# Two parts of the moving operand through one weight load: 512-column matmuls in the FFN and convolution projections

## The chip, the cores and the metric

The kernel runs on one core of a Trainium2 chip. The metric is the device time of one execution in microseconds (us). Before the change it is 1189.55 us, the median of 3 runs (1188.36 to 1194.43).

A core has five engines with a queue each. TensorE (PE) multiplies a stationary operand of 128x128 (the weights, loaded by a separate instruction, PEld) with a moving operand of up to 512 columns and writes into PSUM, a memory of 8 banks with 512 fp32 values in each of 128 partitions. VectorE (DVE), ScalarE (ACT) and GpSimd (POOL) do elementwise work. SyncE (SP) issues the transfers from HBM. An engine takes its instructions strictly in the order of its queue.

## The reference

Four residual layers over 256 positions of width 1024. Each layer is a token mixer (short convolution, recurrent block, latent attention, short convolution) and a SwiGLU FFN of width 2816:

```python
def short_conv_mixer(xn, w_in, w_conv, w_out):
    b_gate, c_gate, h = jnp.split(xn @ w_in, 3, axis=-1)
    y = b_gate * causal_depthwise_conv(c_gate * h, w_conv)
    return y @ w_out

def swiglu_ffn(xn, w_gu, w_down):
    gate, up = jnp.split(xn @ w_gu, 2, axis=-1)
    return (jax.nn.silu(gate) * up) @ w_down

h = x
for i in range(DEPTH):                       # DEPTH = 4
    xn = rms_norm(h, mix_norm[i])
    y = ...                                  # mixer i mod 3
    h = h + y
    h = h + swiglu_ffn(rms_norm(h, ffn_norm[i]), ffn_w_gu[i], ffn_w_down[i])
```

All of it is fp32.

## The kernel before

**Layout.** Activations stand transposed: features on the 128 partitions, the 256 positions (`S`) along the free dimension. The residual stream is `xt`, 8 tiles (`KD`) of 128x256. The FFN's hidden vector is 22 such tiles (`KF`).

**Precision.** An fp32 product is made of three matmuls of a shorter type (fp32r). Each operand is split into a high part (a copy in fp32r) and a low part (what the copy lost): `whi`, `wlo` for weights, `xh`, `xl` for the normalised stream, `yh`, `yl` for the convolution's result, `hh`, `hl` for the hidden vector. `mm3` (L166 to L168) adds high times high, high times low and low times high into the same PSUM columns; the low times low is left out. So each block of 128x128 weights takes three matmuls of 256 columns, each with its own weight load, two of them of the same `whi` block.

**Weights.** `load_w` fetches a tile of 128 x 1024 (four blocks deep, 256 output features wide) on SP's queue, ACT makes `whi` (L79), DVE makes `wlo` (L80). Up to 8 tiles are held ahead; there are 6 raw buffers, 8 of `whi` and 8 of `wlo`, so a new `whi` waits until TensorE has used the tile eight places earlier. Every weight is used once.

**FFN.** The loop over `jp` (11 steps per layer, 44 in all) makes 256 hidden features a step. A step takes four weight tiles: gate and up for the first four blocks of the stream, then gate and up for the last four. Two PSUM banks are in use: bank `j` holds the gate in columns 0 to 255 and the up branch in 256 to 511. Then, for each `j`, DVE multiplies the bank by the norm factor (L966, 512 columns), ACT applies SiLU (L968), POOL multiplies by the up branch (L969), and `split` makes `hh` on ACT (L179) and `hl` on DVE (L180). The down projection is `project_out` in layers 0 to 2 (four output pairs `mp`, each 22 blocks deep and one bank wide) and `project_last` in layer 3, which has the positions as rows. After each pair `mp` one DVE addition of 512 columns brings the bank into `xt` (L293), and `epilogue` makes the new `xh` (ACT, L182), `xl` (DVE, L183), the squares (ACT, L239) and their sum `acc` (POOL, L244) for the next norm.

**Convolution.** The in-projection makes three parts in 12 groups, POOL, ACT and DVE make `y`, and `project_out` multiplies by `w_out`.

**Order.** The framework's scheduler sets each engine's instruction order from the dependencies; the code's own order is a guide to it. The PSUM pool of the projections has six banks (`mm`), a second pool has two (`mi`). A tile taken from the pool gets the bank that was taken six tiles earlier and waits until that one has been read.

Of the kernel before, what the change touches and what calls it, by code (L numbers as in the profile page):

```python
# [16 lines left out]
P = 128  # L17
# [30 lines left out]
KC = 4  # L48
# [5 lines left out]
def tile_trunk(ctx: ExitStack, tc: tile.TileContext, ins: dict, out: bass.AP):  # L54
# [9 lines left out]
    def ps_tile():  # L64
        return psum.tile([P, 512], F32, name="mm")
# [96 lines left out]
    def mm3(ps, a, b, start, stop):  # L162
# [59 lines left out]


    xt = st.tile([P, KD, S], F32, name="xt")
    xh = st.tile([P, KD, S], F32R, name="xh")
    xl = st.tile([P, KD, S], F32R, name="xl")
    acc = st.tile([P, S], F32, name="acc")
    rstd = st.tile([P, S], F32, name="rstd")

# [51 lines left out]
    def project_out(ktiles, rhs, gain, order=None, pss=None):  # L281
# [3 lines left out]
        for mp, k0, k in order or out_order(ktiles):  # L285
# [68 lines left out]

    def short_conv(li, l):
        with tc.tile_pool(name=f"cv{li}", bufs=2) as pool:
            yh = pool.tile([P, KD, S], F32R, name="yh", bufs=1)
            yl = pool.tile([P, KD, S], F32R, name="yl", bufs=1)

            at, rb, pend, g = (0, 1) if li else (2, 3), None, [], {}  # L360

            def conv(jp, cg, hg, bg):
                ch = pool.tile([P, 2, S + CW - 1], F32, name="ch")
                nc.gpsimd.memset(ch[:, :, :CW - 1], 0.0)
                nc.gpsimd.tensor_tensor(ch[:, :, CW - 1:], cg, hg, op=ALU.mult)
                y = pool.tile([P, 2, S], F32, name="y")
                for j in range(2):
                    m = 2 * jp + j

                    def cw(i):  # L370
                        o = o_cw + (l * CW + i) * KD + m
                        return c1[:, o:o + 1]

                    nc.scalar.activation(y[:, j], ch[:, j, 0:S], AF.Copy, scale=cw(0))
                    for i in range(1, CW):
                        nc.vector.scalar_tensor_tensor(y[:, j], ch[:, j, i:i + S], cw(i), y[:, j],
                                                       op0=ALU.mult, op1=ALU.add)
                nc.gpsimd.tensor_tensor(y, y, bg, op=ALU.mult)
                split((yh[:, 2 * jp:2 * jp + 2, :], yl[:, 2 * jp:2 * jp + 2, :]), y)

            for n, (jp, part) in enumerate((jp, part) for jp in range(KD // 2) for part in (1, 2, 0)):
                ps = ps_tile().rearrange("p (a s) -> p a s", s=S)
# [8 lines left out]
                while rb is not None and pend:  # L391
# [2 lines left out]
                    nc.vector.tensor_tensor(g[part], ps, rb, op=ALU.mult)  # L394
                    if part == 0:
                        conv(jp, g[1], g[2], g[0])
            project_out(KD, lambda k: (yh[:, k, :], yl[:, k, :]),
                        o_ffn + li * KD)

    def late_params(late):  # L400
        c2, (o_lcw, o_lcb, o_gab, o_gxb, o_lam) = columns("c2", [
# [536 lines left out]

    def ffn(li):
        with tc.tile_pool(name=f"ff{li}", bufs=2) as pool:  # L940
            hh = pool.tile([P, KF, S], F32R, name="hh", bufs=1)
            hl = pool.tile([P, KF, S], F32R, name="hl", bufs=1)
            rb = None
            for jp in range(KF // 2):
                if li == DEPTH - 1 and jp == 0:
                    xr = pool.tile([P, 2, D], F32, name="xr", bufs=1)
                if li == DEPTH - 1 and 4 <= jp < 4 + KD // 2:
                    by_position(xr, jp - 4)
                if (li, jp) == (0, 2):
                    late.extend(late_params(pool))  # L950
                pss = [ps_tile().rearrange("p (a s) -> p a s", s=S) for _ in range(2)]
                for k0 in range(0, KD, KC):
                    w = next_ws(2)
                    if jp == 0 and k0:
                        dg = norm_sums()
                    for k in range(KC):
                        for i, (hi, lo) in enumerate(w):
                            for j, ps in enumerate(pss):
                                sl = slice(j * P, (j + 1) * P)
                                mm3(ps[:, i, :], (hi[:, k, sl], lo[:, k, sl]), xk(k0 + k),  # L960
                                    start=(k0 + k == 0 and i == 0), stop=(k0 + k == KD - 1))
                for j, ps in enumerate(pss):
                    f = 2 * jp + j
                    rb = rb or norm_bcast(dg)
                    gu = pool.tile([P, 2, S], F32, name="gu")
                    nc.vector.tensor_tensor(gu, ps, rb, op=ALU.mult)  # L966
                    s = pool.tile([P, S], F32, name="s")
                    nc.scalar.activation(s, gu[:, 0], AF.Silu)  # L968
                    nc.gpsimd.tensor_tensor(s, s, gu[:, 1], op=ALU.mult)  # L969
                    split((hh[:, f, :], hl[:, f, :]), s)  # L970
            hidden = lambda k: (hh[:, k, :], hl[:, k, :])
            if li == DEPTH - 1:
                project_last(KF, hidden, xr)
            else:
                project_out(KF, hidden, o_mix + (li + 1) * KD)

    late = []
    short_conv(0, 0)
# [36 lines left out]
```

## Time and profile before

| | |
|---|---|
| median of 3 runs | 1189.55 us |
| profiled execution, its time | 1188.12 us |
| profiled execution, its span | 1186.3 us |
| TensorE busy | 1156.7 us (98%), 9475 matmuls |
| VectorE busy | 805.6 us (68%) |
| ScalarE busy | 609.0 us (51%) |
| GpSimd busy | 259.8 us (22%) |
| HBM read | 202.04 MB, 171 GB/s over the span |
| mean granted clock of TensorE | 0.993 |

The span is the stretch between the first and the last instruction of the trace; 1.8 us lie around it. A matmul's recorded duration (280 to 290 ns for 256 columns) covers its passage through the pipeline, so matmuls overlap; what one costs is the distance between the starts of two that follow each other. In the FFN's steps a matmul starts every 120 ns for stretches of tens of microseconds.

### The profile page before, as it was taken

How to read it: one execution, taken by the hardware profiler on the slowest of the kernel's cores; microseconds unless marked ns; L12 is line 12 of the kernel's file. 1: busy time of each engine (PE TensorE's matmuls, PEld its weight loads, DVE VectorE, ACT ScalarE, POOL GpSimd, SP SyncE). 2: the span in 40 equal slices, each digit the busy share in tenths (PEclk: the TensorE clock that was granted, in tenths of full speed). 3: DMA queues.
4: the chain of work that ended last, by engine and by line, in shares of the span. 5: the costliest groups of instructions: out<-in, count | busy, mean ns of one | idle time of the engine just before them, and what ended most of it. 6: DMA issues, size and time to landing. Idle time of an engine off the chain costs nothing.

```text
span 1186.3 us, 23326 instructions
## 1 busy us (share of the span) xinstructions
PE 1156.7 (98%) x9475; PEld 1146.8 (97%) x9475; DVE 805.6 (68%) x1147; ACT 609.0 (51%) x919; POOL 259.8 (22%) x231
## 2 busy tenths in 40 slices
PE   7999999999998999999999899999999999999998
PEld 6999999999898999999998799999999999999998
DVE  6787886655789767675558866767556787676651
ACT  6345444444697645444458654444444444454530
POOL 5311122213324222121105011212111111221200
PEclk8999999999999999999999899999999999999999
DMA  8665565656642765655653245565666565556560
GB/s 289 197 194 179 169 188 179 183 182 186 198 131 83 236 187 176 191 169 186 181 174 101 89 125 177 180 193 170 181 193 188 179 186 171 182 173 182 161 192 19
DMA packets 211483, 204.60 MB, mean 172 GB/s; under 512 B 12777, under 2 KB 210096, under 8 KB 211376
## 3 DMA queue, kind: packets, MB, share of 16 engines
q1 hardware_dynamic: 211202, 203.05, 55.9%
q8 instruction: 74, 1.21, 0.4%
q14 instruction: 33, 0.27, 0.1%
q10 hardware_dynamic: 174, 0.06, 0.0%
HBM read 202.04 MB, written 1.05 MB: 171 GB/s over the span
## 4 chain that ended last, share of the span: by engine, by line
PE 87%; DVE 5%; ACT 3%; POOL 2%; DMA 1%; issue 1%; SPq 0%; ACTq 0%; DVEq 0%; POOLq 0%
PE mm L167 28%; PE mm L166 28%; PE mm L168 28%; DVE wlo L80 2%; POOL acc L244 1%; DVE xb L489 1%; ACT whi L79 1%; DVE xb L546 1%; PE mi L660 0%; DMA posi<-in_positions 0%; DMA wraw<-in_conv_w_in 0%; DVE xl L183 0%; ACT sm L891 0%; DMA rows<-in_ffn_norm 0%; PE mm L171 0%
## 5 line engine op out<-in xcount | busy, mean ns | idle before, releaser
L80 DVE TENSOR_TENSOR wlo<-wraw,whi 128x1024 fp32r<-128x1024 f32 (+2 forms) x389 | 497.8, 1300 | 183.9 <-ACT whi L79 180.1
L79 ACT ACTIVATE whi<-wraw 128x1024 fp32r<-128x1024 f32 (+2 forms) x397 | 396.1, 1025 | 390.9 <-PE mm L167 321.7
L166 PE MATMUL mm<-xh,whi 128*128 128x256 f32 x2000 | 569.3, 285 | 2.5 <-ACT xh L182 2.5
L167 PE MATMUL mm<-xl,whi 128*128 128x256 f32 x2000 | 567.5, 284 | 1.1 <-DVE xl L183 1.1
L168 PE MATMUL mm<-xh,wlo 128*128 128x256 f32 x2000 | 567.0, 284 | 0.0
L166 PEld LDWEIGHTS mm<-xh,whi 128*128 128x128 f32 x2000 | 384.9, 193 | 3.2 <-ACT xh L182 2.9
L167 PEld LDWEIGHTS mm<-xl,whi 128*128 128x128 f32 x2000 | 385.1, 193 | 2.0 <-DVE xl L183 1.8
L168 PEld LDWEIGHTS mm<-xh,wlo 128*128 128x128 f32 x2000 | 385.0, 193 | 0.0
L969 POOL TENSOR_TENSOR s<-s,gu 128x256 f32<-128x256 f32 x88 | 114.2, 1315 | 395.4 <-ACT s L968 395.4
L167 PE MATMUL mm<-hl,whi 128*128 128x256 f32 x528 | 149.4, 283 | 0.0
L168 PE MATMUL mm<-hh,wlo 128*128 128x256 f32 x528 | 149.2, 282 | 0.0
L166 PE MATMUL mm<-hh,whi 128*128 128x256 f32 x528 | 148.0, 280 | 0.0
L966 DVE TENSOR_TENSOR gu<-mm,rstd 128x512 f32<-128x512 f32 x88 | 56.7, 685 | 101.3 <-PE mm L168 101.3
L166 PEld LDWEIGHTS mm<-hh,whi 128*128 128x128 f32 x528 | 100.4, 190 | 0.0
L168 PEld LDWEIGHTS mm<-hh,wlo 128*128 128x128 f32 x528 | 99.1, 188 | 0.0
L167 PEld LDWEIGHTS mm<-hl,whi 128*128 128x128 f32 x528 | 98.8, 187 | 0.0
L179 ACT ACTIVATE hh<-s 128x256 fp32r<-128x256 f32 x88 | 36.6, 417 | 85.8 <-POOL s L969 85.8
L244 POOL TENSOR_TENSOR acc<-acc,sq 128x256 f32<-128x256 f32 x48 | 50.5, 1051 | 114.2 <-ACT sq L239 111.9
L180 DVE TENSOR_TENSOR hl<-s,hh 128x256 fp32r<-128x256 f32 x88 | 57.8, 658 | 12.2 <-ACT hh L179 12.0
L167 PE MATMUL mm<-yl,whi 128*128 128x256 f32 x208 | 59.5, 286 | 3.0 <-DVE yl L180 3.0
L166 PE MATMUL mm<-yh,whi 128*128 128x256 f32 x208 | 59.2, 285 | 0.5 <-ACT yh L179 0.5
L168 PE MATMUL mm<-yh,wlo 128*128 128x256 f32 x208 | 59.5, 286 | 0.0
(290 smaller groups left out, 1224.0 us busy)
## 6 DMA issues: line engine op xcount, KB each, us to landing
wraw<-in_ffn_w_gu SPq DMA_DIRECT2D x176, 512.0 KB, 4.5
wraw<-in_ffn_w_down SPq DMA_DIRECT2D x80, 512.0 KB, 4.5
wraw<-in_conv_w_in SPq DMA_DIRECT2D x48, 512.0 KB, 4.6
wraw<-in_lru_w_in SPq DMA_DIRECT2D x20, 512.0 KB, 4.1
wraw<-in_conv_w_out SPq DMA_DIRECT2D x16, 512.0 KB, 4.0
wraw<-in_ffn_w_down SPq DMA_DIRECT2D x16, 256.0 KB, 3.4
wraw<-in_lru_w_out SPq DMA_DIRECT2D x8, 512.0 KB, 3.4
wraw<-in_mla_w_o SPq DMA_DIRECT2D x8, 512.0 KB, 3.4
```

The costliest lines, as they stand in the source:

```text
L79: nc.scalar.activation(hi[:, :n], raw[:, :n], AF.Copy)
L80: (eng or nc.vector).tensor_tensor(lo[:, :n], raw[:, :n], hi[:, :n].bitcast(F32), op=ALU.subtract)
L166: nc.tensor.matmul(ps, ah, bh, start=start, stop=False, skip_group_check=True)
L167: nc.tensor.matmul(ps, ah, bl, start=False, stop=False, skip_group_check=True)
L168: nc.tensor.matmul(ps, al, bh, start=False, stop=stop, skip_group_check=True)
L179: nc.scalar.activation(hi, src, AF.Copy)
L180: nc.vector.tensor_tensor(lo, src, hi.bitcast(F32), op=ALU.subtract)
L244: nc.gpsimd.tensor_tensor(acc, acc, sq[:, i], op=ALU.add)
L489: nc.vector.scalar_tensor_tensor(xb[:, n], rc[:, j, i:i + S], cw(i), xb[:, n], op0=ALU.mult, op1=ALU.add)
L546: nc.vector.tensor_tensor_scan(xb[:, n], aa[np_][:, j], xb[:, n], 0.0, op0=ALU.mult, op1=ALU.add)
L966: nc.vector.tensor_tensor(gu, ps, rb, op=ALU.mult)
L969: nc.gpsimd.tensor_tensor(s, s, gu[:, 1], op=ALU.mult)
```

## The change

A new helper `mm2` replaces `mm3` in the FFN's gate and up projections, the FFN's down projection of layers 0 to 2 and the convolutions' out projection. High and low part of the moving operand now stand in one tile (`xp`, `yp`, `hp`, with a dimension of 2), and one matmul of 512 columns sends both past `whi`: high times high goes into columns 0 to 255 of a bank, the product of the low part into columns 256 to 511. A second matmul of 256 columns adds `wlo` times high into the second half. Whoever reads the bank must add its halves. So a result of 128 features takes a whole bank instead of half of one: a gate and up step holds four banks, a pair `mp` of `project_wide` two. The recurrent block, the attention, the convolution's in-projection and layer 3's down projection keep `mm3`.

```diff
+    def mm2(ps, a, b, start, stop):
+        nc.tensor.matmul(ps, a[0], b, start=start, stop=False, skip_group_check=True)
+        nc.tensor.matmul(ps[:, 1], a[1], b[:, 0], start=False, stop=stop, skip_group_check=True)
...
-    xh = st.tile([P, KD, S], F32R, name="xh")
-    xl = st.tile([P, KD, S], F32R, name="xl")
+    xp = st.tile([P, 2, KD, S], F32R, name="xp")
+    xh, xl = xp[:, 0], xp[:, 1]
...
+    def project_wide(ktiles, rhs, gain):
+        for mp in range(KD // 2):
+            pss = [ps_tile().rearrange("p (a s) -> p a s", s=S) for _ in range(2)]
+            for k0 in range(0, ktiles, KC):
+                hi, lo = next_w()
+                for i in range(hi.shape[1]):
+                    for j, ps in enumerate(pss):
+                        sl = slice(j * P, (j + 1) * P)
+                        mm2(ps, (hi[:, i, sl], lo[:, i, sl]), rhs(k0 + i),
+                            start=(k0 + i == 0), stop=(k0 + i == ktiles - 1))
+            for j, ps in enumerate(pss):
+                for a in range(2):
+                    xs = xt[:, 2 * mp + j, :]
+                    nc.vector.tensor_tensor(xs, xs, ps[:, a], op=ALU.add)
+            epilogue(2 * mp, 2, gain)
...
-            project_out(KD, lambda k: (yh[:, k, :], yl[:, k, :]),
-                        o_ffn + li * KD)
+            project_wide(KD, lambda k: yp[:, :, k, :], o_ffn + li * KD)
...
-                    for k in range(KC):
-                        for i, (hi, lo) in enumerate(w):
-                            for j, ps in enumerate(pss):
+                    for i, (hi, lo) in enumerate(w):
+                        for j in range(2):
+                            if k0 == 0:
+                                pss[i][j] = ps_tile().rearrange("p (a s) -> p a s", s=S)
+                        for k in range(KC):
+                            for j, ps in enumerate(pss[i]):
                                 sl = slice(j * P, (j + 1) * P)
-                                mm3(ps[:, i, :], (hi[:, k, sl], lo[:, k, sl]), xk(k0 + k),
-                                    start=(k0 + k == 0 and i == 0), stop=(k0 + k == KD - 1))
-                for j, ps in enumerate(pss):
-                    f = 2 * jp + j
-                    rb = rb or norm_bcast(dg)
-                    gu = pool.tile([P, 2, S], F32, name="gu")
-                    nc.vector.tensor_tensor(gu, ps, rb, op=ALU.mult)
-                    s = pool.tile([P, S], F32, name="s")
-                    nc.scalar.activation(s, gu[:, 0], AF.Silu)
-                    nc.gpsimd.tensor_tensor(s, s, gu[:, 1], op=ALU.mult)
-                    split((hh[:, f, :], hl[:, f, :]), s)
+                                mm2(ps, (hi[:, k, sl], lo[:, k, sl]), xp[:, :, k0 + k, :],
+                                    start=(k0 + k == 0), stop=(k0 + k == KD - 1))
+                rb = rb or norm_bcast(dg)
+                gu = pool.tile([P, 2, 2, S], F32, name="gu")
+                for i in range(2):
+                    for j in range(2):
+                        ps = pss[i][j]
+                        nc.scalar.copy(gu[:, i, j], ps[:, 1])
+                        nc.vector.tensor_tensor(gu[:, i, j], ps[:, 0], gu[:, i, j], op=ALU.add)
+                    nc.vector.tensor_tensor(gu[:, i], gu[:, i], rb, op=ALU.mult)
+                s = pool.tile([P, 2, S], F32, name="s")
+                nc.scalar.activation(s, gu[:, 0], AF.Silu)
+                nc.gpsimd.tensor_tensor(s, s, gu[:, 1], op=ALU.mult)
+                f2 = slice(2 * jp, 2 * jp + 2)
+                split((hp[:, 0, f2, :], hp[:, 1, f2, :]), s)
...
-                project_out(KF, hidden, o_mix + (li + 1) * KD)
+                project_wide(KF, lambda k: hp[:, :, k, :], o_mix + (li + 1) * KD)
```

The scheduler's order shows what moves. First TensorE, in the middle of a gate and up step: `mm_` is a PSUM bank, `whi_` and `wlo_` a weight tile; these rows are the kernel before, the last three of them the up branch.

```order
L166 MATMUL mm_6190<-xh_88,whi_6058 128x256
L167 MATMUL mm_6190<-xl_89,whi_6058 128x256
L168 MATMUL mm_6190<-xh_88,wlo_6059 128x256
L166 MATMUL mm_6191<-xh_88,whi_6058 128x256
L167 MATMUL mm_6191<-xl_89,whi_6058 128x256
L168 MATMUL mm_6191<-xh_88,wlo_6059 128x256
L166 MATMUL mm_6190<-xh_88,whi_6064 128x256
L167 MATMUL mm_6190<-xl_89,whi_6064 128x256
L168 MATMUL mm_6190<-xh_88,wlo_6065 128x256
```

The same place in the changed kernel, TensorE from the gate's last block of a weight tile to the up branch's first (its lines are L173 and L174):

```order
L173 MATMUL mm_4674<-xp_88,whi_4473 128x512
L174 MATMUL mm_4674<-xp_88,wlo_4474 128x256
L173 MATMUL mm_4675<-xp_88,whi_4473 128x512
L174 MATMUL mm_4675<-xp_88,wlo_4474 128x256
L173 MATMUL mm_4692<-xp_88,whi_4479 128x512
L174 MATMUL mm_4692<-xp_88,wlo_4480 128x256
L173 MATMUL mm_4693<-xp_88,whi_4479 128x512
L174 MATMUL mm_4693<-xp_88,wlo_4480 128x256
```

Three matmuls of 256 columns became one of 512 and one of 256, and gate (4674, 4675) and up (4692, 4693) have banks of their own, worked tile by tile and no longer block by block.

Second DVE's queue over one gate and up step, before: `gu_` is the normalised gate and up pair, `hl_` the low part of the hidden vector.

```order
L80 TENSOR_TENSOR wlo_6255<-wraw_6252,whi_6254 128x1024
L80 TENSOR_TENSOR wlo_6261<-wraw_6258,whi_6260 128x1024
L966 TENSOR_TENSOR gu_6312<-mm_6190,rstd_91 128x512
L966 TENSOR_TENSOR gu_6319<-mm_6191,rstd_91 128x512
L80 TENSOR_TENSOR wlo_6331<-wraw_6328,whi_6330 128x1024
L80 TENSOR_TENSOR wlo_6337<-wraw_6334,whi_6336 128x1024
L180 TENSOR_TENSOR hl_4948<-s_6314,hh_4947 128x256
L180 TENSOR_TENSOR hl_4948<-s_6321,hh_4947 128x256
```

DVE's queue over one such step in the changed kernel, beginning with the gate:

```order
L992 TENSOR_TENSOR gu_4754<-mm_4674,gu_4754 128x256
L80 TENSOR_TENSOR wlo_4773<-wraw_4770,whi_4772 128x1024
L992 TENSOR_TENSOR gu_4754<-mm_4675,gu_4754 128x256
L993 TENSOR_TENSOR gu_4754<-gu_4754,rstd_90 128x512
L992 TENSOR_TENSOR gu_4754<-mm_4692,gu_4754 128x256
L80 TENSOR_TENSOR wlo_4779<-wraw_4776,whi_4778 128x1024
L992 TENSOR_TENSOR gu_4754<-mm_4693,gu_4754 128x256
L993 TENSOR_TENSOR gu_4754<-gu_4754,rstd_90 128x512
L80 TENSOR_TENSOR wlo_4821<-wraw_4818,whi_4820 128x1024
L186 TENSOR_TENSOR hp_4428<-s_4765,hp_4428 128x512
L80 TENSOR_TENSOR wlo_4827<-wraw_4824,whi_4826 128x1024
```

Four additions of 256 columns are new, the weight splits now stand one by one between them, and the two subtractions at the end became one of 512 columns.

Third ACT's queue over the same step of the changed kernel (before, it held four `whi`, two SiLU and two `hh`, in pairs):

```order
L991 COPY gu_4754<-mm_4674 128x256
L79 ACTIVATE whi_4772<-wraw_4770 128x1024
L991 COPY gu_4754<-mm_4675 128x256
L991 COPY gu_4754<-mm_4692 128x256
L79 ACTIVATE whi_4778<-wraw_4776 128x1024
L991 COPY gu_4754<-mm_4693 128x256
L995 ACTIVATE s_4765<-gu_4754 128x512
L79 ACTIVATE whi_4820<-wraw_4818 128x1024
L185 ACTIVATE hp_4428<-s_4765 128x512
L79 ACTIVATE whi_4826<-wraw_4824 128x1024
```

Four copies out of PSUM are new, and the last `whi` stands behind `hp`, which waits for POOL's product.

## Rows read from the trace of the kernel before

**Rows 1.** Page, busy time by engine, and the chain that ended last:
```profile
PE 1156.7 (98%) x9475; PEld 1146.8 (97%) x9475; DVE 805.6 (68%) x1147; ACT 609.0 (51%) x919; POOL 259.8 (22%) x231
...
PE 87%; DVE 5%; ACT 3%; POOL 2%; DMA 1%; issue 1%; SPq 0%; ACTq 0%; DVEq 0%; POOLq 0%
```

**Rows 2.** Groups of TensorE's instructions (busy us, mean ns | idle before):
```profile
L166 PE MATMUL mm<-xh,whi 128*128 128x256 f32 x2000 | 569.3, 285 | 2.5 <-ACT xh L182 2.5
...
L166 PE MATMUL mm<-hh,whi 128*128 128x256 f32 x528 | 148.0, 280 | 0.0
...
L166 PE MATMUL mm<-yh,whi 128*128 128x256 f32 x208 | 59.2, 285 | 0.5 <-ACT yh L179 0.5
```

**Rows 3.** TensorE in a gate and up step (start us, duration us):
```profile
199.75 0.28 PE L166 MATMUL mm<-xh,whi 128*128 128x256 f32 x1
...
201.91 0.28 PE L166 MATMUL mm<-xh,whi 128*128 128x256 f32 x1
```

**Rows 4.** TensorE in the attention, 256 columns and then 512:
```profile
635.76 0.28 PE L166 MATMUL mm<-cth,whi 128*128 128x256 f32 x1
...
636.71 0.28 PE L168 MATMUL mm<-cth,wlo 128*128 128x256 f32 x1
636.83 0.39 PE L171 MATMUL mm<-whi,cth 128*128 128x512 f32 x1
...
637.99 0.40 PE L173 MATMUL mm<-whi,ctl 128*128 128x512 f32 x1
```

**Rows 5.** TensorE in the attention, a little earlier, 512 columns:
```profile
629.62 0.40 PE L172 MATMUL mm<-wlo,cth 128*128 128x512 f32 x1
...
630.55 0.39 PE L173 MATMUL mm<-whi,ctl 128*128 128x512 f32 x1
```

**Rows 6.** Groups of DVE's instructions, shapes apart:
```profile
L80 DVE TENSOR_TENSOR wlo<-wraw,whi 128x1024 fp32r<-128x1024 f32 x358 | 473.3, 1343 | 161.7 <-ACT whi L79 157.9 <-PE mm L167 2.9
...
L293 DVE TENSOR_TENSOR xt<-xt,mm 128x512 f32<-128x512 f32 x28 | 19.1, 681 | 4.5 <-PE mm L168 4.5
...
L180 DVE TENSOR_TENSOR yl<-y,yh 128x512 fp32r<-128x512 f32 x8 | 5.9, 740 | 5.0 <-ACT yh L179 5.0
...
L351 DVE TENSOR_TENSOR ot<-mm,xr 128x256 f32<-128x256 f32 x8 | 3.1, 420 | 17.2 <-PE mm L168 17.2
...
L773 DVE TENSOR_TENSOR ks<-ks,fk 128x512 f32<-128x512 f32 x4 | 2.6, 680 | 0.0
```

**Rows 7.** Groups of ACT's instructions, shapes apart:
```profile
L79 ACT ACTIVATE whi<-wraw 128x1024 fp32r<-128x1024 f32 x366 | 376.6, 1055 | 359.7 <-PE mm L167 303.5 <-PE mm L168 22.7 <-issue 22.0
...
L179 ACT ACTIVATE yh<-y 128x512 fp32r<-128x512 f32 x8 | 5.1, 632 | 15.9 <-POOL ch L364 10.0 <-POOL y L378 5.9
...
L757 ACT ACTIVATE ks<-mm 128x256 f32<-128x256 f32 x8 | 3.1, 390 | 1.2 <-PE mm L173 1.2
```

**Rows 8.** Groups of POOL's instructions, 512 columns:
```profile
L378 POOL TENSOR_TENSOR y<-y,g 128x512 f32<-128x512 f32 x8 | 13.1, 1638 | 30.4 <-DVE g L394 19.6 <-DVE y L376 10.8
L365 POOL TENSOR_TENSOR ch<-g,g 128x512 f32<-128x512 f32 x8 | 10.4, 1295 | 65.1 <-DVE g L394 65.1
```

**Rows 9.** Timeline of one gate and up step, DVE and POOL:
```profile
457.65 2.90 DVE L80 TENSOR_TENSOR wlo<-wraw,whi 128x1024 fp32r<-128x1024 f32 x2
...
458.42 2.72 POOL L969 TENSOR_TENSOR s<-s,gu 128x256 f32<-128x256 f32 x2 [8.79 <-ACT s L968]
```

**Rows 10.** Busy us in two stretches: us, PE, PEld, DVE, ACT, POOL, clock, DMA:
```profile
100.00:110.00 10.00, 10.00 (x86) 10.00 (x85) 8.00 (x9) 5.41 (x9) 3.21 (x4) 1.00 0.63 193
...
440.00:452.00 12.00, 12.00 (x102) 12.00 (x101) 8.25 (x9) 5.94 (x9) 2.73 (x2) 1.00 0.60 194
```

**Rows 11.** TensorE early in the first FFN:
```profile
122.80 0.70 PE L264 MATMUL mi<-dg,ones 128*128 128x256 f32 x2 [0.77 <-DVE dg L258]
```

**Rows 12.** TensorE as the second convolution begins:
```profile
904.13 0.52 PEld L250 LDWEIGHTS mi<-ones,acc 128*128 128x128 f32 x4 [0.27 <-POOL acc L244]
```

**Rows 13.** Chain of waits as the recurrent block begins (start us, us, what):
```profile
309.27 2.19 DVE rsy L189
...
315.39 0.34 DVE rstd L265
315.75 0.70 DVE rc L478
```

More of the change, by code (lines that the diff above doesn't have):

```diff
@@ L356, in short_conv @@
         with tc.tile_pool(name=f"cv{li}", bufs=2) as pool:
-            yh = pool.tile([P, KD, S], F32R, name="yh", bufs=1)
-            yl = pool.tile([P, KD, S], F32R, name="yl", bufs=1)
+            yp = pool.tile([P, 2, KD, S], F32R, name="yp", bufs=1)
             at, rb, pend, g = (0, 1) if li else (2, 3), None, [], {}
@@ L378, in conv @@
                 nc.gpsimd.tensor_tensor(y, y, bg, op=ALU.mult)
-                split((yh[:, 2 * jp:2 * jp + 2, :], yl[:, 2 * jp:2 * jp + 2, :]), y)
+                split((yp[:, 0, 2 * jp:2 * jp + 2, :], yp[:, 1, 2 * jp:2 * jp + 2, :]), y)
             for n, (jp, part) in enumerate((jp, part) for jp in range(KD // 2) for part in (1, 2, 0)):
@@ L940, in ffn @@
         with tc.tile_pool(name=f"ff{li}", bufs=2) as pool:
-            hh = pool.tile([P, KF, S], F32R, name="hh", bufs=1)
-            hl = pool.tile([P, KF, S], F32R, name="hl", bufs=1)
+            hp = pool.tile([P, 2, KF, S], F32R, name="hp", bufs=1)
             rb = None
@@ L950, in ffn @@
                     late.extend(late_params(pool))
-                pss = [ps_tile().rearrange("p (a s) -> p a s", s=S) for _ in range(2)]
+                pss = [[None] * 2 for _ in range(2)]
                 for k0 in range(0, KD, KC):
@@ L971, in ffn @@
-            hidden = lambda k: (hh[:, k, :], hl[:, k, :])
+                    for i, (hi, lo) in enumerate(w):
[4 more added lines that the diff above has]
+                            for j, ps in enumerate(pss[i]):
+                                sl = slice(j * P, (j + 1) * P)
+                                mm2(ps, (hi[:, k, sl], lo[:, k, sl]), xp[:, :, k0 + k, :],
+                                    start=(k0 + k == 0), stop=(k0 + k == KD - 1))
@@ L972, in ffn @@
+                nc.scalar.activation(s, gu[:, 0], AF.Silu)
+                nc.gpsimd.tensor_tensor(s, s, gu[:, 1], op=ALU.mult)
+                f2 = slice(2 * jp, 2 * jp + 2)
+                split((hp[:, 0, f2, :], hp[:, 1, f2, :]), s)
             if li == DEPTH - 1:
-                project_last(KF, hidden, xr)
+                project_last(KF, lambda k: (hp[:, 0, k, :], hp[:, 1, k, :]), xr)
             else:
-                project_out(KF, hidden, o_mix + (li + 1) * KD)
+                project_wide(KF, lambda k: hp[:, :, k, :], o_mix + (li + 1) * KD)
```

## The prediction

> **What bounds the kernel now.** I read the page's busy times and its chain first [rows 1]. TensorE is busy 98% of the span and holds 87% of the chain that ended last; the rest is spread over the start and two mixers. So the kernel costs what TensorE's instruction stream costs, and the first question is what one matmul costs there.
>
> That is the distance between starts, not the recorded duration. In a gate and up step 18 distances fill 201.91 - 199.75 = 2.16 us, 120 ns for 256 columns [rows 3]. For 512 columns the attention's value projection has rows: five distances fill 637.99 - 636.83 = 1.16 us, 232 ns [rows 4]; three quarters of a microsecond earlier and in the same code four fill 0.93 us, 232.5 ns [rows 5]. So twice the columns cost less than twice the time: 240 - 232.5 = 7.5 ns a matmul do not grow with the columns. That is what the change can collect. The 256-column matmuls just ahead of those rows stand 0.95 / 8 = 119 ns apart [rows 4], a little closer than in the FFN; scaled by 120 / 119 the 512 columns would take 234.5 ns there.
>
> The granted clock is 1.00 in the FFN's stretches [rows 10], the upper of its two levels, and TensorE stays without a pause, so no term comes from the clock.
>
> **TensorE's part.** Blocks that change: 44 steps x 32 = 1408 in gate and up (they are among the 2000 of `xh`), 528 in the down projections, 128 of the 208 with `yh` [rows 2]; together 2064. Each loses one matmul of 256 columns with its weight load and turns another into 512. Before: 3 x 120 = 360 ns. After: 232.5 + 120 = 352.5 ns at best, 354.5 with the scaled value; I take 353.5. 2064 x 6.5 ns = 13.4 us less (10.9 to 15.5). What no row shows is a moving operand in two runs: the 512 columns of the rows are contiguous, the new ones are 256 of the high part and 256 of the low part some KB away. Its bounds are 240 ns, where the second run starts anew like a matmul of its own and nothing is gained, and, since a gain below the contiguous row has no reason, 232.5. I take the row's value, because within a run nothing differs.
>
> A gate and up step falls from 96 x 0.120 = 11.52 us to 32 x 0.3535 = 11.31 us. Everything that follows must fit into that.
>
> **What the other engines get.** Nearest rows are those of the same shape [rows 6, 7, 8]. DVE per step: four weight splits of 1.343, four additions out of PSUM of 0.42 (new), two products of 0.68, one subtraction of 0.74, in sum 9.15 us, where it had 8.25 x 11.52 / 12 = 7.9 [rows 10]. ACT: four `whi` of 1.055, four copies of 0.39 (new), SiLU and `hp` of 0.63 each, 7.0 us (5.94 in 12 before). POOL: one product of 1.3 to 1.64 us for two that took 2.72 [rows 9]. All fit into 11.31 us, DVE with 81%.
>
> Busy shares are not enough, since the queues are strict and wait on each other. I set t = 0 where TensorE ends a step. ACT copies up 0 by 0.45, makes a `whi` by 1.5, copies up 1 by 1.9. DVE finishes the gate's second addition at 0.4 and its product at 1.1, adds up 0 by 1.5, splits a weight until 2.8, adds up 1 and multiplies by 3.9. POOL then takes until 5.5, `hp` until 6.2, the last `whi` until 7.2, its split until 8.6. The next gate is ready on TensorE at 8.5, so its copy ends at 8.9 and the first addition at 9.4, then a split until 10.8 and the second addition at 11.2, which closes the round. A gate's banks are read out by 0.4, and the next step's up branch wants them a quarter of a step in, at 2.8: 2.4 us to spare. The up banks are wanted a whole step later. The split that ends at 8.6 belongs to a tile that TensorE reads at 11.3 + 2.8 = 14.1. So I cost the steady steps at nothing. The cover has an end: the round POOL, `hp`, `whi`, three splits behind it, four additions, two products is 1.64 + 0.63 + 1.06 + 4.03 + 1.68 + 1.36 = 10.4 us, and beyond 11.3 TensorE would follow it.
>
> **Stage ends.** After each of the five wide projections four additions of 0.42 = 1.7 us replace one of 0.68 [rows 6]: 1.0 us later before `xp`, the squares and the next norm. It shows only where TensorE waits already. At the second convolution its weight load waited 0.27 us for the sum of squares [rows 12]; ACT's first half can start after the third addition, so I add 0.4 (0 to 1.0). At the recurrent block the chain runs over DVE [rows 13]: 1.0. At the others no row shows a wait; 0. While the convolutions project, DVE is busy 8.0 of 10 us [rows 10] and gets 1.0 more per 5.7: nearly full, but the weights are eight tiles ahead and it lasts 23 us, 0 to 1 us each.
>
> In the first FFN the wait of 0.77 us for `dg` [rows 11] goes, since `dg` now stands ahead of the instruction that waits for the positions; but the rope and decay tables share DVE with the new additions there. I take +1.0 in sum (-0.8 to +4).
>
> Sum: -13.4 + 0.4 + 1.0 + 1.0 = -11.0 us. The profiled execution took 1188.1, so 1177.1. The median of the runs lies 1.4 above that execution; I give 1178.
>
> **Rivals.**
> A second run that costs like a new matmul: 512 columns take 240 ns, no gain on TensorE, and 2.4 us for the ends: 1190.5. For it: no row has such an operand. Against: the runs are long, and the columns themselves are what 512-column rows mostly pay for.
>
> A smaller fixed part: if the longer distances hold (237 ns after scaling), 3 ns a block remain, 6.2 us, and the time is 1188.1 - 6.2 + 2.4 = 1184. For it: the two lengths give 120 - 7.5 = 112.5 ns for 256 columns, so the fixed part is a small difference of large numbers. The Trainium skill (TensorE: Matmul & The Clock Gate, "Wait — 56ns, not 53.3ns?") puts the fixed cost of a matmul at about 2.5 ns over its columns at 2.4 GHz; by that 2064 matmuls less would give an estimated 5.2 us. The trace disagrees with it at both lengths: 120 and 232.5 ns against 109 and 216.
>
> DVE's round becomes the bound, and the kernel is slower. Where it decides: POOL's product reads two tiles while DVE splits a weight right behind its own product, and before the two plainly held each other up: two splits took 2.90 us and two products of half the size 2.72 in the same stretch [rows 9]. If the one product still takes 2.72 from the end of DVE's product, the round is 11.5 us, with a tenth for each of four handovers 11.9, and 0.6 us x 40 steps = 24 us come back: 1201. Against: with 1.64 it is 10.4, and alone the shape took 1.3 [rows 8]; it decides from about 2.2 us on. The Trainium skill (SBUF — State Buffer, "Who interferes with whom") says that a DVE instruction with both inputs in SBUF and a GpSimd instruction that reads SBUF exclude each other for a whole instruction, whoever starts first. The rows agree (2.90 and 2.72 together), and by it a split that gets in first would push the product back by one split, to about 2.5.
>
> **Chances.** Forecast 0.70, no gain 0.10, smaller part 0.07, DVE's round 0.13. About 0.5% (5.9 us) can be told from no change here: below 1183.6 is faster, above 1195.5 slower. The forecast's own range is 1173 to 1184 (the term's bounds, and the ends' 0 to 6). Faster 0.70; the same 0.17 (no gain and the smaller part); slower 0.13. The range that holds 8 in 10 goes from 1170 to 1192.
>
> **What will show it.** In a gate and up step two starts of L173 should stand 353 ns apart, and the step 11.3 us; a distance of 360 means the second run costs. TensorE should have no wait for L992 in the steady steps; if it has, or if the step is 11.5 to 12 us with DVE without idle time, the round bounds. TensorE's busy share stays at 97 to 98% with 7400 matmuls. A wait at L256 of about 0.7 us and a later recurrent block show the stage ends. I am wrong if the step doesn't shorten, or if the ends cost more than 6 us together.

## The result: 1172.9 us, 1.4% faster

| | before | after |
|---|---|---|
| median, runs of one chip | 1190.82 us (1188.36 to 1194.43) | 1172.91 us (1170.91 to 1174.60) |
| profiled execution, its time and span | 1188.12, 1186.3 us | 1171.75, 1170.0 us |

The ratio is 0.9861, 95% interval 0.9845 to 0.9877. A second comparison gave 0.9876 (0.9853 to 0.9899). The forecast was 1178 us, 1170 to 1192.

The page's busy times of the kernel after, beside [rows 1]:

```profile
PE 1137.4 (97%) x7411; PEld 1034.4 (88%) x7411; DVE 883.3 (75%) x1339; ACT 652.1 (56%) x1007; POOL 202.2 (17%) x187
```

TensorE still sets the time, with 2064 matmuls less. Its weight loads fell from 97% to 88% of the span: for the first time there is room between them.

Groups of instructions after, shapes apart (busy us, mean ns | idle before), beside [rows 2] and [rows 6 to 8]:

```profile
L173 PE MATMUL mm<-xp,whi 128*128 128x512 f32 x1408 | 494.3, 397 | 3.0 <-DVE xt L299 1.9 <-DVE xp L189 1.0
...
L173 PE MATMUL mm<-hp,whi 128*128 128x512 f32 x528 | 185.0, 393 | 0.0
...
L173 PE MATMUL mm<-yp,whi 128*128 128x512 f32 x128 | 45.0, 393 | 0.0
...
L992 DVE TENSOR_TENSOR gu<-mm,gu 128x256 f32<-128x256 f32 x176 | 73.6, 419 | 24.7 <-ACT gu L991 24.7
L993 DVE TENSOR_TENSOR gu<-gu,rstd 128x512 f32<-128x512 f32 x88 | 60.9, 692 | 2.6
...
L991 ACT COPY gu<-mm 128x256 f32<-128x256 f32 x176 | 64.4, 367 | 109.2 <-PE mm L174 109.2
...
L996 POOL TENSOR_TENSOR s<-s,gu 128x512 f32<-128x512 f32 x44 | 60.0, 1365 | 437.6 <-DVE gu L993 389.7 <-ACT s L995 13.0 <-DVE ld_p L447 12.1
```

1408 + 528 + 128 = 2064 blocks; additions, copies and products cost nearly what the nearest rows of before had. In 3.0 us of idle time on the first line the only waits are for L299 and L189; no wait for L992 shows.

What a block costs now, again from starts. TensorE in layer 1's gate and up, then in layer 3's (start us, duration us):

```profile
459.69 0.40 PE L173 MATMUL mm<-xp,whi 128*128 128x512 f32 x1
459.92 0.28 PE L174 MATMUL mm<-xp,wlo 128*128 128x256 f32 x1
460.04 0.39 PE L173 MATMUL mm<-xp,whi 128*128 128x512 f32 x1
...
461.77 0.40 PE L173 MATMUL mm<-xp,whi 128*128 128x512 f32 x1
...
1079.81 0.40 PE L173 MATMUL mm<-xp,whi 128*128 128x512 f32 x1
1080.04 0.28 PE L174 MATMUL mm<-xp,wlo 128*128 128x256 f32 x1
...
1081.58 0.40 PE L173 MATMUL mm<-xp,whi 128*128 128x512 f32 x1
```

Layer 1: six blocks in 2.08 us, 347 ns each. Layer 3: five blocks in 1.77 us, 354 ns. Over the 2064 blocks of the trace a start of 512 columns is followed after 232.9 ns on average, one of 256 after 116.5 (distances above 300 ns left out): 349.4 ns a block, against 360 before. A steady step takes 11.09 us (346.5 ns a block) in most of layers 1 and 2 and 11.31 us (353.3 ns) in those of layer 3 that don't also hold the transposes of `by_position`; it was 11.52 in all of them.

Stage by stage (from the first matmul of a stage to the first of the next; us):

| stage | before | after | difference |
|---|---|---|---|
| start and first convolution's in-projection | 86.88 | 86.23 | -0.65 |
| the two convolution out projections | 46.08 | 44.88 | -1.20 |
| gate and up, layer 0 | 128.70 | 123.95 | -4.75 |
| down, layers 0 to 2 | 190.08 | 184.82 | -5.26 |
| recurrent block, in | 72.34 | 73.82 | +1.48 |
| recurrent block, out | 33.62 | 34.85 | +1.23 |
| gate and up, layer 1 | 129.30 | 127.17 | -2.13 |
| attention; gate and up, layer 2 | 234.19 | 231.62 | -2.57 |
| second convolution, in | 70.30 | 69.96 | -0.34 |
| gate and up, layer 3 | 129.31 | 126.89 | -2.42 |
| down, layer 3, and end | 65.53 | 65.77 | +0.24 |
| sum | 1186.33 | 1169.96 | -16.37 |

2064 x (360 - 349.4) = 21.9 us were earned and 5.5 given back. Layer 1 shows it best: 352 blocks at 347 ns should save 4.6 us, and it saved 2.1. TensorE as that FFN opens, the kernel after (in brackets the wait and what ended it):

```profile
405.56 0.28 PE L174 MATMUL mm<-xp,wlo 128*128 128x256 f32 x1
406.21 0.50 PE L173 MATMUL mm<-xp,whi 128*128 128x512 f32 x1 [0.37 <-DVE xt L299]
...
406.89 0.28 PE L174 MATMUL mm<-xp,wlo 128*128 128x256 f32 x1
408.73 0.50 PE L173 MATMUL mm<-xp,whi 128*128 128x512 f32 x1 [1.56 <-DVE xt L299]
...
409.42 0.28 PE L174 MATMUL mm<-xp,wlo 128*128 128x256 f32 x1
410.74 0.50 PE L173 MATMUL mm<-xp,whi 128*128 128x512 f32 x1 [1.04 <-DVE xp L189]
```

Three pauses between starts, 0.65 + 1.84 + 1.32 = 3.8 us (before: 0.99 and 0.78). DVE at that time:

```profile
405.48 0.68 DVE L299 TENSOR_TENSOR xt<-xt,mm 128x512 f32<-128x512 f32 x1
406.08 1.21 DVE L80 TENSOR_TENSOR wlo<-wraw,whi 128x1024 fp32r<-128x1024 f32 x1
...
408.00 0.67 DVE L299 TENSOR_TENSOR xt<-xt,mm 128x512 f32<-128x512 f32 x1
408.60 1.21 DVE L80 TENSOR_TENSOR wlo<-wraw,whi 128x1024 fp32r<-128x1024 f32 x1
409.74 1.82 DVE L189 SCALAR_TENSOR_TENSOR xp<-xt,c,xp 128x256 fp32r<-128x256 f32 x2
```

TensorE resumes right behind each L299 and behind the first L189 of the last pair. L299 is the addition that brings the recurrent block's result out of its banks; two of them stand behind weight splits, and the pair that is finished last (`mp` 1) is the one whose blocks 2 and 3 the FFN needs second.

Two more places. The recurrent block's start, then the FFN of layer 2:

```profile
306.04 0.28 PE L168 MATMUL mm<-xp,wlo 128*128 128x256 f32 x1
307.44 0.70 PE L270 MATMUL mi<-dg,ones 128*128 128x256 f32 x2 [1.12 <-DVE dg L264]
...
704.41 0.28 PE L174 MATMUL mm<-xp,wlo 128*128 128x256 f32 x1
705.72 0.60 PE L256 MATMUL mi<-ones,acc 128*128 128x1 f32 x4 [1.03 <-POOL acc L250]
```

The norm's DVE chain ends 0.9 us later against TensorE than before (a pause of 1.40 us for 0.49), and at 705.72 the sum of squares is awaited, which it was not.

### The profile page after: what moved, and what is told of

Its sections match the earlier page's. It is cut to its first block, busy times and chain, and to the rows that moved or that the text cites. A ratio compares the mean times of both kernels' runs of the same rounds, so it can differ in the third digit from the quotient of the medians.

```text
span 1170.0 us, 19307 instructions
## 1 busy us (share of the span) xinstructions
PE 1137.4 (97%) x7411; PEld 1034.4 (88%) x7411; DVE 883.3 (75%) x1339; ACT 652.1 (56%) x1007; POOL 202.2 (17%) x187
## 4 chain that ended last, share of the span: by engine, by line
PE 62%; ACT 1%; DVE 1%; POOL 0%; issue 0%; ACTq 0%; POOLq 0%
PE mm L173 29%; PE mm L174 14%; PE mm L166 6%; PE mm L167 6%; PE mm L168 6%; PE mi L681 0%; ACT sm L912 0%; DVE wlo L80 0%; PE mm L177 0%; PE mm L179 0%; PE mm L178 0%; POOL acc L250 0%; DVE ktl L189 0%; PE mi L270 0%; PE mi L350 0%
## 5 line engine op out<-in xcount | busy, mean ns | idle before, releaser
L173 PE MATMUL mm<-xp,whi 128*128 128x512 f32 x1408 | 494.3, 397 | 3.0 <-DVE xt L299 1.9
L174 PE MATMUL mm<-xp,wlo 128*128 128x256 f32 x1408 | 392.0, 278 | 0.0
L173 PEld LDWEIGHTS mm<-xp,whi 128*128 128x128 f32 x1408 | 264.2, 188 | 66.2 <-DVE xt L299 2.6
L174 PEld LDWEIGHTS mm<-xp,wlo 128*128 128x128 f32 x1408 | 265.0, 188 | 0.1
L173 PE MATMUL mm<-hp,whi 128*128 128x512 f32 x528 | 185.0, 393 | 0.0
L166 PE MATMUL mm<-xp,whi 128*128 128x256 f32 x592 | 169.9, 287 | 0.9 <-ACT xp L188 0.9
L167 PE MATMUL mm<-xp,whi 128*128 128x256 f32 x592 | 169.0, 285 | 0.9 <-DVE xp L189 0.9
L168 PE MATMUL mm<-xp,wlo 128*128 128x256 f32 x592 | 168.6, 285 | 0.0
L174 PE MATMUL mm<-hp,wlo 128*128 128x256 f32 x528 | 147.3, 279 | 0.0
L173 PEld LDWEIGHTS mm<-hp,whi 128*128 128x128 f32 x528 | 98.9, 187 | 23.7
L167 PEld LDWEIGHTS mm<-xp,whi 128*128 128x128 f32 x592 | 114.9, 194 | 1.5 <-DVE xp L189 1.4
L166 PEld LDWEIGHTS mm<-xp,whi 128*128 128x128 f32 x592 | 114.8, 194 | 1.4 <-ACT xp L188 1.1
L168 PEld LDWEIGHTS mm<-xp,wlo 128*128 128x128 f32 x592 | 114.8, 194 | 0.0
L174 PEld LDWEIGHTS mm<-hp,wlo 128*128 128x128 f32 x528 | 98.9, 187 | 0.0
L992 DVE TENSOR_TENSOR gu<-mm,gu 128x256 f32<-128x256 f32 x176 | 73.6, 419 | 24.7 <-ACT gu L991 24.7
```

The lines of the kernel that those rows point to most:

```text
L166: nc.tensor.matmul(ps, ah, bh, start=start, stop=False, skip_group_check=True)
L173: nc.tensor.matmul(ps, a[0], b, start=start, stop=False, skip_group_check=True)
L174: nc.tensor.matmul(ps[:, 1], a[1], b[:, 0], start=False, stop=stop, skip_group_check=True)
L992: nc.vector.tensor_tensor(gu[:, i, j], ps[:, 0], gu[:, i, j], op=ALU.add)
```

## The experiments

Two questions were open: why the gain on TensorE was half as large again as forecast, and where the 5.5 us went. For the first, theory F (the forecast's): each matmul pays a fixed part beside its columns. Theory W: 256 columns stream in 116 ns, and their 120 came from weight loads that hardly fit beside them.

**e1, the merge alone taken back.**

```diff
-        nc.tensor.matmul(ps, a[0], b, start=start, ...)
+        nc.tensor.matmul(ps[:, 0], a[0], b[:, 0], start=start, ...)
+        nc.tensor.matmul(ps[:, 1], a[0], b[:, 1], start=False, ...)
```

> The changed kernel, but each 512-column matmul is issued as two of 256 (high part into the first half of the bank, low part into the second). Banks, evacuation, additions and order stay as changed. Theory C (the gain comes from the merged matmul): the distances between starts go back to 120 ns, 360 ns a block instead of 349.4, 2064 x 10.6 = 21.9 us more: about 1195 us, gate and up steps 11.5 us, slower than the kernel before by what the new stage ends cost (some 5 us). Theory S (the gain comes from the new structure: tile by tile order, separate banks, merged SiLU and product): most of the gain stays, 1173 to 1180 us.

1192.2 us, ratio to before 1.0024 (1.0006 to 1.0041). TensorE in layer 1:

```profile
460.01 0.28 PE L173 MATMUL mm<-xp,whi 128*128 128x256 f32 x1
...
462.89 0.28 PE L173 MATMUL mm<-xp,whi 128*128 128x256 f32 x1
```

24 distances in 2.88 us: 120 ns, steps of 11.52 us. Theory S is out: all of the gain is the merged matmul, and the new structure without it costs a quarter of a percent, 2.6 us (some 5 were expected). What comes back here is a matmul together with its weight load, so the run doesn't tell which of the two is paid for.

**e2 and e3, each part alone.** e2 keeps `mm2` in gate and up and takes `project_out` for the rest; e3 the reverse.

> Only gate and up use the 512-column matmul (1408 of 2064 blocks); down and convolution out projections are as before, one addition of 512 columns a pair. Theory C: 656 blocks x about 10.3 ns = 6.8 us come back, and the later start of the recurrent block (1.5 us over the kernel before) goes away: about 1173 + 6.8 - 1.5 = 1178 us. If the additions at the stage ends cost much more than that: at or below 1176 us. The opening of the FFN after the recurrent block keeps its 3.8 us of waits, since they come from the FFN's four banks.

> Only the down projections of layers 0 to 2 and the convolutions' out projections use the 512-column matmul (656 blocks); gate and up are as before. Theory C: 656 x 10.3 = 6.8 us less than before, 1.5 us back at the recurrent block: about 1191 - 6.8 + 1.5 = 1186 us. The opening of the FFN after the recurrent block falls back to the 1.8 us of waits that it had before.

1180.4 us for e2 (ratio 0.9908, 0.9879 to 0.9938) and 1180.5 for e3 (0.9912, 0.9888 to 0.9937). Each missed, by 2 us upwards and 5.5 downwards. In e2 the FFN of layer 1 took 130.64 us, more than before the change: it ran its steps at 11.31, not 11.09, and its opening had the 3.8 us of pauses and more, below. In e3 that opening has pauses of 2.1 us between starts, near the 1.8 of before; its three down projections save 5.2 us, as in the full change, and 2.4 us come from a recurrent out projection of 31.26 us. That stage takes 31.3 to 34.9 us in the profiles of this case, whatever the kernel (the changed kernel itself 34.85 in one and 33.61 in another), so these 2.4 us, and the 1.23 in the table above, are not put down to the change.

**e4, other widths in the kernel before.**

```diff
+ if not first and li == 0:   # 320 columns
+     bh, bl = (x.rearrange("p k s -> p (k s)")[:, kk*S:kk*S+320] for x in (xh, xl))
+ if not first and li in (1, 2):
+     n = 192 if li == 1 else 128
+     bh, bl, o = bh[:, :n], bl[:, :n], o[:, :n]
+ if not first and li == 3:   # third matmul
+     nc.tensor.matmul(o[:64], wl[:, :64], bh, ...)
```

> The kernel before with other widths in gate and up, after the first block of each bank: layer 0 with 320 moving columns, layer 1 with 192, layer 2 with 128, layer 3 with 256 columns but only 64 stationary columns in the third matmul (columns that fall away or are added make other sums than the reference's). Theory F (each matmul pays a fixed part of 7.5 ns beside 0.44 ns a column): distances of 148 ns at 320 columns, 92 at 192, 64 at 128, 120 in layer 3. Theory W (0.454 ns a column, and a floor of about 120 ns that a matmul with a weight load of 128 columns cannot pass): 145 ns at 320, 110 to 120 at 192 and at 128 alike, and in layer 3, if the floor is the length of the load, about 116 to 118 ns on the distance of the short load; if the floor is the issue of two instructions, 120 there too.

One execution took 1207.1 us; only the distances count. TensorE's starts with 192, 128 and 320 columns, and then its matmuls and loads (PEld) in layer 3:

```profile
499.84 0.27 PE L166 MATMUL mm<-xh,whi 128*128 128x192 f32 x1
...
502.97 0.27 PE L167 MATMUL mm<-xl,whi 128*128 128x192 f32 x1
...
779.79 0.27 PE L167 MATMUL mm<-xl,whi 128*128 128x128 f32 x1
...
780.91 0.28 PE L168 MATMUL mm<-xh,wlo 128*128 128x128 f32 x1
...
199.87 0.31 PE L166 MATMUL mm<-xh,whi 128*128 128x320 f32 x1
...
202.94 0.31 PE L166 MATMUL mm<-xh,whi 128*128 128x320 f32 x1
...
1079.88 0.28 PE L970 MATMUL mm<-xh,whi 128*128 128x256 f32 x1
...
1081.97 0.28 PE L970 MATMUL mm<-xh,whi 128*128 128x256 f32 x1
...
1079.88 0.19 PEld L971 LDWEIGHTS mm<-xl,whi 128*128 128x128 f32 x1
1080.00 0.14 PEld L972 LDWEIGHTS mm<-xh,wlo 128*64 128x64 f32 x1
```

192 columns: 28 distances in 3.13 us, 112 ns. 128 columns: 10 in 1.12 us, 112 ns. A third of the columns less changes nothing: there is a floor near 112 ns, and F, which has no floor (92 and 64 ns), is out for them. Both widths lie on the floor, so they don't tell whether a wider matmul has a fixed part. 320 columns do: 21 distances in 3.07 us, 146 ns, and 146.7 on average over layer 0, between the two theories. From 256 to 320 columns of the same triples that is (146.7 - 120) / 64 = 0.417 ns a column, which leaves 13 ns of the 120. By this estimate a fixed part is there, larger than forecast, and a pair of 512 and 256 would take 768 x 0.417 + 2 x 13.3 = 347 ns, as in the steps of 11.09 us. It doesn't fit everything: triples of 512 columns would take 227 ns each, and the attention's took 232.

With a load of 64 columns for every third matmul, 18 distances of the same 256 columns take 2.09 us, 116 ns for 120. The FFN's triples kept 120 ns in every other profile, so the load's width seems to matter; but layer 3's down projection has 117.4 ns with full loads, and that the load sets the floor is not shown, since no run varied it at 128 or 192 columns. The Trainium skill (TensorE: Matmul & The Clock Gate, "Back-to-back issue gap") says that in a stream of loads and matmuls the spacing is set by both. These distances agree; its figure for 128 columns, 81 ns, does not, where 112 were measured.

**e5, other orders of the changed kernel.** Layer 1: big, big, small, small; layer 2: contiguous operand; layer 3: eight big, eight small.

```diff
- for k in range(KC):
-     for j in range(2):
-         mm2(...)
+ kj = [(k, j) for k in range(KC) for j in range(2)]
+ if li == 3:
+     for x in kj: big(*x)
+     for x in kj: small(*x)
```

> The changed kernel with other orders or operands in gate and up. Layer 0 is unchanged. Layer 1 goes 512, 512, 256, 256 (two features' big matmuls, then their two small ones). Layer 2 gives the 512-column matmul a contiguous operand (two neighbouring blocks of the high part, so the sums are not the reference's). Layer 3 sends the eight big matmuls of a weight tile first, then its eight small ones. Theory W (a 256-column matmul has 116 ns of columns; its 120 in a stretch of them comes from the floor of 111 that each weight load sets, which a 512-column neighbour takes off): layer 3 has 120 ns inside its runs of small ones, so 232.6 + 120 = 352.5 ns a block, steps of 11.28 us; layer 1 about 350 ns, 11.2 us; layer 2 the same distances as layer 0. Theory R (the two-run operand is what costs): layer 2 faster than layer 0. Theory F (a fixed part a matmul): 352.5 ns everywhere.

Layer 3's runs of eight (x8 are eight matmuls of one row):

```profile
1080.81 1.12 PE L992 MATMUL mm<-xp,wlo 128*128 128x256 f32 x8
1081.76 2.00 PE L988 MATMUL mm<-xp,whi 128*128 128x512 f32 x8
1083.60 1.11 PE L992 MATMUL mm<-xp,wlo 128*128 128x256 f32 x8
```

Eight small ones in 0.95 us: 119 ns among themselves, where alternation has 116. Eight big ones in 1.84 us, 230 ns, where alternation has 233. The small ones are as W says; the big ones make up for them, so the block came to 349 ns, steps of 11.17 us for the 11.28 that W expected. Layer 1's order gave 11.15 us. So W misses too. Within the 2% that lie between the two step times of the changed kernel itself (11.09 and 11.31 us), a block costs the same in every order. The starts book the gain now on one matmul and now on the other, and only their sum can be relied on. F's 352.5 ns everywhere is out as a size; a fixed part of 10 to 13 ns is not. Layer 2, contiguous, 11.09 us in every steady step, like the changed kernel's layer 2: the operand in two runs costs nothing, R is out. (The whole execution took 1171.7 us.)

**e7, how much room DVE has.**

```diff
+ for _ in range(li):
+     nc.vector.tensor_tensor(gu[:, 1], gu[:, 1], gu[:, 1], op=ALU.max)
```

> The changed kernel with extra VectorE work in each gate and up step, behind the product with the norm factor: none in layer 0, one maximum of the up branch with itself (512 columns, 0.68 us) in layer 1, two in layer 2, three in layer 3. VectorE is busy 9.2 us of a step of 11.1 in the changed kernel. Theory of the round (product on GpSimd, hidden vector, last weight, three splits, four additions, two products, 10.1 us with GpSimd's measured 1.3): 10.8 us in layer 1, hidden; 11.5 us a step in layer 2; 12.2 in layer 3. Theory of busy time alone: 9.9, 10.6 and 11.2 us, so that layer 1 and 2 keep 11.1 to 11.3 us and layer 3 comes out at 11.3.

The operation took 690 ns, the one execution 1179.2 us. Layers 1 and 2 kept 11.31 and 11.09 us. A step of layer 2 (us, PE, PEld, DVE, ACT, POOL, granted clock, DMA):

```profile
771.00:782.09 11.09, 11.09 (x66) 9.70 (x66) 9.99 (x14) 6.47 (x11) 1.30 (x1) 1.00 0.62 191
```

With two more operations a step nothing is lost, and GpSimd's products follow each other every 11.09 us, as TensorE's steps do; the round's sum had said 11.5. In layer 3, with three, the products come every 12.2 us from the fourth to the tenth:

```profile
1072.76 2.12 POOL L998 TENSOR_TENSOR s<-s,gu 128x512 f32<-128x512 f32 x1 [10.09 <-DVE gu L995]
1084.97 2.11 POOL L998 TENSOR_TENSOR s<-s,gu 128x512 f32<-128x512 f32 x1 [10.09 <-DVE gu L995]
```

That is the round's 12.2, and not the 11.3 of busy time alone: DVE was busy 10.0 us of such a step. TensorE, at 11.3 to 11.7 us a step, ran ahead of it, and waited for the first time in the tenth step, which took 12.2 us:

```profile
PE mm L173 <- DVE gu L992: 1.3, 2, 0.6
```

(us in all, times, longest.) So it is the round that bounds, though its sum came out too high in layer 2.

**e6a and e6b, the opening after the recurrent block.** e6a finishes the output pairs in order; e6b takes four weight splits off DVE.

```diff
- (0, 8, 2), (2, 8, 2), (3, 8, 2), (1, 8, 2)]
+ (0, 8, 2), (1, 8, 2), (2, 8, 2), (3, 8, 2)]
```

> The changed kernel with the recurrent block's last weight tiles in the order of output pairs 0, 1, 2, 3 instead of 0, 2, 3, 1, so that the four blocks that the FFN reads first are ready first. Theory B (the FFN's opening waits because it wants more banks than the recurrent block has given back): the waits of 3.8 us at the opening stay within half a us. Theory X (it waits because gate and up, worked tile by tile, run out of finished blocks of the stream): they fall to below 2 us, and the stage from recurrent block to FFN shortens by 1.5 to 3 us.

> The changed kernel with the low parts of the first four weight tiles of layer 1's FFN made by GpSimd, not VectorE. In the trace VectorE has no idle time from 399 to 411 us, and its additions that bring the recurrent result out of PSUM stand behind four such splits of 1.22 us. Theory Q (the opening's waits are VectorE's queue): the last of these additions ends 2 to 4 us sooner and the waits of 3.8 us fall below 1.5. Theory G (GpSimd, slower and excluding VectorE while it reads, hands the time back): waits stay at 3 us or more, or TensorE waits for the weights instead.

e6a: 1168.4 us in one execution, of which 3.6 come from its recurrent out projection, 31.28 us for 34.85; the three pauses became one of 0.57 us and one of 1.46 for the sum of squares, and the stage 125.37 us for 127.17. X had the pauses below 2 us, and they are 2.0; the stage is 1.8 us shorter, inside its 1.5 to 3. X is right in the main, B falls: the banks were awaited because TensorE, out of finished blocks, had been given the next step's gate (16 matmuls, two blocks of the stream into four banks, stand ahead of the first pause). e6b: 1175.0 us, stage 131.31. TensorE's waits in e6b at the opening:

```profile
PE mm L173 <- DVE xt L299: 2.9, 2, 2.5
PE mm L173 <- DVE xp L189: 0.9, 2, 0.6
```

Longer than the 1.9 of the changed kernel. A split on GpSimd takes 2.4 to 2.9 us there, and DVE's additions came no sooner; G, not Q.

**The order, timed, and a wider version.**

> The changed kernel once more, so that the two versions below stand against it on one chip: a ratio to before of 0.984 to 0.988.

> The changed kernel with the recurrent block's last tiles in the order 0, 1, 2, 3. Theory X (blocks of the stream in the wrong order) with the clock: the opening's 3.8 us of pauses are gone in every execution, and with them the stretch at half clock that some executions showed there: 2 to 5 us below the changed kernel, a ratio to before of 0.981 to 0.985. Theory B (banks): the single profile was a lucky one, same ratio as the changed kernel.

> The version with the new order, and beside it the 512-column matmul in two more places: the second convolution's in-projection (192 blocks, each result in a bank of its own, a copy on ScalarE and an addition on VectorE before the product with the norm factor), and layer 3's down projection, whose first half of the features now takes 512 columns of weights (88 triples of 256 become 44 of 512, without any new addition). Theory W: 192 x 10.6 = 2.0 us and 44 x (720 - 698) = 1.0 us less, ratio to before 0.9785 to 0.983; stage of the in-projection 68 us instead of 70, last stage 64.8 instead of 65.8. Rival: VectorE (8.5 of 10 us busy early in that stage) cannot take two additions more per group, and the stage gets no shorter than 70 us.

| | median us | ratio to before |
|---|---|---|
| changed kernel | 1173.28 (1172.64 to 1173.97) | 0.9876 (0.9853 to 0.9899) |
| with the new order | 1170.40 (1166.72 to 1174.06) | 0.9851 (0.9826 to 0.9875) |
| order, and two more places | 1171.83 (1171.33 to 1172.32) | 0.9861 (0.9838 to 0.9884) |

The order is 2.9 us ahead in the medians, but the intervals overlap, so a gain in the whole time is not shown clear of the noise. In the traces it is: the stage takes 125.4 to 125.8 us in the three profiles with the new order, and 127.17 and 128.67 in the two of the changed kernel. Busy us at the opening, the changed kernel and then the new order (us, PE, PEld, DVE, ACT, POOL, granted clock, DMA):

```profile
406.00:409.00 3.00, 1.46 (x8) 0.77 (x6) 3.00 (x6) 1.76 (x4) 1.39 (x2) 1.00 0.53 168
409.00:412.00 3.00, 1.59 (x7) 1.19 (x8) 3.00 (x4) 1.43 (x3) 2.76 (x4) 1.00 0.67 188
412.00:415.00 3.00, 3.00 (x11) 2.40 (x11) 0.38 (x2) 1.06 (x1) 0.78 (x1) 0.52 0.46 161
```

```profile
406.00:409.00 3.00, 2.04 (x12) 1.33 (x10) 3.00 (x4) 1.82 (x3) 2.73 (x3) 1.00 0.70 225
409.00:412.00 3.00, 3.00 (x19) 2.68 (x20) 2.69 (x6) 1.49 (x3) 0.00 (x0) 1.00 0.43 129
```

After six us in which TensorE was busy about half, the clock stood at 0.52, the lower level of 1.2 GHz, and a pair took 0.64 us instead of 0.35. The first profile of the changed kernel had the same pauses and kept 1.00; this one and those of e2, e5, e6b and e7 lost the clock there, and their first step took 16.9 to 18.2 us where the first profile's had taken 15.5. None of the three profiles with the new order lost it.

The wider version missed its 0.9785 to 0.983 and lost what it won. Its in-projection went from 69.96 to 68.70 us, but the out projection behind it from 22.44 to 24.69, since TensorE waited there:

```profile
PE mm L175 <- DVE yp L188: 2.0, 1, 2.0
```

The additions delay the last `yp` on DVE. And layer 3's down projection took 65.97 us for 65.77: its triples of 256 already ran at 117.4 ns, before the change too, and 512 columns at 234.3 are no less.

## Why the prediction was right, and where its sizes were off

**TensorE's part.** The mechanism held: one matmul less per block, with its load, is the gain (e1), 232.5 ns was taken for 512 columns and 232.9 measured, and the operand in two runs costs what a contiguous one does (e5). The mis-sized term is what a block gives back, 6.5 ns forecast and 10.6 measured: -21.9 us instead of -13.4, outside the term's own bounds. (The smaller of them, 10.9 us, should read 11.4, 2064 x 5.5 ns.) By the starts it is the other matmul, kept at 120 ns, that measured 116.5. The 353.5 ns of the forecast are right where steps take 11.31 us (353.3) and too many where they take 11.09 (346.5); that a block has two costs stood in no row. "7.5 ns a matmul do not grow with the columns" was too small a part: 256 columns of the FFN were set against 512 of the attention, whose price doesn't lie on one line with the FFN's own 256 and 320 columns (13 ns by e4). Whether the part belongs to the matmul or to its load, and why 256 columns take 116.5 ns beside 512 and 120 among themselves, stays open. That PEld was busy 97% beside PE 98% [rows 1] was a hint that loads count, and the prediction read past it.

**Steady steps at nothing.** Right. One step, busy us in the same columns, beside [rows 10]:

```profile
460.00:471.09 11.09, 11.09 (x66) 9.70 (x65) 9.19 (x12) 6.47 (x10) 1.29 (x1) 1.00 0.61 192
```

DVE 9.19 (9.15 forecast), ACT 6.47 (7.0), POOL 1.29 (1.3 to 1.64), TensorE without a pause. DVE's round as a bound did not come. In a steady step the product got in first and the split waited:

```profile
467.18 1.29 POOL L996 TENSOR_TENSOR s<-s,gu 128x512 f32<-128x512 f32 x1 [9.81 <-DVE gu L993]
...
467.46 2.10 DVE L80 TENSOR_TENSOR wlo<-wraw,whi 128x1024 fp32r<-128x1024 f32 x1 [0.45 <-ACT whi L79]
```

2.10 us for 1.22 alone. That is the exclusion the prediction cited from the Trainium skill (SBUF — State Buffer, "Who interferes with whom"), with the roles the other way round: it cost DVE 0.9 us that DVE had. Who starts first did not decide it, though: in layer 1 of e7 the product took 2.1 us a step, beside one DVE operation more, and TensorE still did not wait.

**Stage ends.** Forecast +2.4 us, measured 5.5, of which 1.2 is the recurrent out projection's own spread. The recurrent block: 1.0 forecast, 1.5 measured, on the chain that was named. The second convolution: 0.4 forecast; no cost. The first FFN: the wait for `dg` went as forecast; the +1.0 for tables beside additions did not show, it saved 4.75 us. Missed were the FFN of layer 1, some 2.4 us, and that of layer 2, 1.3 us at L256. "At the others no row shows a wait" was the wrong question there: gate and up tile by tile use up the first two blocks of the stream in half the time that block by block did, so a wait that was small could grow. For layer 1 e6a shows it; for layer 2 no run tested it.

**Rivals.** No gain (e5, layer 2) and the smaller part (349.4 ns measured) are out; DVE's round bears two operations more a step, 1.4 us, and not three (e7). The errors of the two sizes, 8.5 us too little gain and 3.1 too little cost, partly cancelled; the time lies 5 us under the forecast and inside the range. That is in part luck: with the gain as measured and the ends as forecast the same sum gives some 1169.5, below the range.

## What to carry to other kernels

Where weight loads are busy nearly all of the span, sending more columns through one load gained more here than the difference of two single rows suggested: 10.6 ns a block for 7.5. Such a merge is priced best by the whole block, in the place and the shapes that it will have, since the starts can book the same cost on either of two neighbours. When a loop is turned so that it uses fewer inputs per unit of time, look at what its first pass finds ready, and order the producer's last tiles by the consumer's first reads. Idle stretches of TensorE at such an opening can cost twice, by the pause and by the clock after it, as in five of the six profiles in which gate and up with 512 columns met the old order of the producer.

## What was not expected of the hardware

Steady pairs of gate and up run in one of two repeating patterns: starts 231, 112, 233, 118 ns apart (two pairs in 693 ns, steps of 11.09 us) or 233, 117, 241, 120, 236, 113 (three in 1060 ns, steps of 11.31). The same code in the same layer ran in the one in some profiles and in the other in others, and stays in it for tens of us: layer 0 of the changed kernel ended at 11.09 in one profile and at 11.31 in the other. The pairs of the down projections kept 350 ns in every profile. Triples of 256 have such patterns too, 120 ns on average in the FFN and 117.4 in layer 3's down projection. What chooses the pattern stays open; no run aimed at it. It is worth up to 2.4 us a layer.
